# Scores of far keys by residue modulo 4, with a softmax in two parts, in a conformer block on one core

## The chip, the cores and the metric

The kernel runs on one core of a Trainium2 chip. The core has a matrix engine (TensorE, PE in the profile, with its weight loads shown apart as PEld), a vector engine (DVE), a scalar engine (ACT), a general engine (POOL) and a sync engine (SP) that issues most DMA transfers. Each engine works through its own list of instructions in order; they meet by semaphores. The metric is the device time of one execution in microseconds (us), as the median of several runs.

## The reference

One block in float32 on 1024 tokens of 1024 channels: a gated causal convolution branch and an attention branch side by side, their gated sum through `w_out`, then a gated feed-forward part. The attention is what the change touches. It has 16 heads of 64 and three groups (window, dilation); each group has its own softmax, and the three outputs are mixed by the softmax of their log-sums:

```python
DILATION_GROUPS = ((128, 1), (512, 4), (2048, 16))
...
for window, dilation in DILATION_GROUPS:
    o_g, lse_g = dilated_window_attention(q, k, v, slopes, window, dilation)
    outs.append(o_g)
    lses.append(lse_g)
mix = jax.nn.softmax(jnp.stack(lses), axis=0)
o = jnp.einsum('gbsh,gbshd->bshd', mix, jnp.stack(outs))
```

Within a group a query sees the keys whose distance to it is a multiple of the dilation, from 0 up to the window; scores get a linear penalty, slope times distance. Mixing by log-sums makes the three groups one softmax in which a key counts once for each group that holds it. So a query sees every key up to distance 128, every fourth up to 512, and every sixteenth beyond.

## The kernel before

All large products run as three matmuls of 32-bit operands split into a high and a low part (`split`: ACT copies the high part with `Copy`, DVE subtracts it from the source to get the low part). The stages follow each other: normalisation and the first gated products, q, k and v, gates by a block scheme with fewer products, attention, merging, `w_out`, the feed-forward part.

**The attention stage** goes head by head over 128-token query blocks i = 0 to 7. It is one hand-ordered loop (`tc.manual_schedule` for ACT, DVE and PE) over *slots*, one for each head, half and block; eight slots make a head, and `at % 8` is called the *place* here. POOL and SP are not ordered by hand: the scheduler decides their order from the dependences. A slot does, in this order:

- `score`: query block i against the key blocks 0 to i, (i+1) x 128 columns, as two matmuls (high and low part of the keys, `kh` and `kl`; the partitions of `q` hold its high and its low part, 64 each). Then one DVE operation subtracts the score from the mask row, writes the result to `p` in SBUF and its minimum to `st`, with a short readout of that accumulator. One mask tile `m` of 1024 columns a head holds, at a shifted offset for each block, the penalty and the logarithm of the count.
- `share` of the slot before: reciprocal on DVE, then POOL scales `p` by it.
- `fill(FRONT[at % 8])` steps of other work for PE: `gates` is a generator in which each step is three matmuls of 512 columns of a gate or of the convolution's output product. `FRONT` and `BEHIND` hold ten steps a head.
- `flip` for the slot `BACK` = 5 before: PE transposes the 128x128 blocks of one key block into a PSUM bank `pp`, ACT copies to `ph`, DVE subtracts to `pl`. In the second half a slot flips two key blocks.
- `weigh` of what the slot before flipped: two matmuls, values as the stationary operand, into the output bank `o`; after the last, `result` copies `o` out on ACT and SP stores it in two pieces of 128 KB.
- `powers`: ACT takes the exponential of `p` in place with the sum in `st` (and a readout).
- `fill(BEHIND[at % 8])`.

`head(h + 1)` fetches q, kh and kl in six transfers of 256 KB, and the mask, a head ahead into buffers that go in pairs; `values` fetches the values, 512 KB. A key block counts 36 times a head: 1 + 2 + ... + 8. After the last slot come a few slots without scores; there the attention output of the finished half is fetched back for the merge. A DMA's landing is told by one of eight semaphores, and a transfer is issued only when the one that had the same semaphore before it has landed.

The lines of before that the steps name: L911 and L912 scores, L916 mask and minimum with its readout, L921 exponential with its readout, L924 reciprocal, L925 the scaling on POOL, L931 transposes, L82 and L83 the two halves of a split, L945 and L946 weighing, L954 the copy of the output, L956 its stores, L114 to L116 the matmuls of fill steps and other products, L242 and L243 copy and store of the convolution's product, L731 a scaled activation of the convolution branch that writes every second float.

Of the kernel before, what the change touches and what calls it, by code (L numbers as in the profile page):

```python
# [35 lines left out]
FRONT = (1, 1, 0, 0, 0, 1, 0, 1)  # L36
BEHIND = (1, 1, 1, 1, 0, 1, 1, 0)
BACK = 5
# [18 lines left out]
def block_kernel(ctx: ExitStack, tc: tile.TileContext, x, xT, x0, g2, pack, mask,  # L57
# [20 lines left out]
    qkg = cst.tile([P, 1], F32, name="qkg")  # L78

# [74 lines left out]
    dv = [dr.tile([P, 8, 8, P], F32R, name=f"dv{i}") for i in range(2)]  # L154
# [145 lines left out]
    if True:  # L300
# [434 lines left out]
        def head(h):  # L735
# [4 lines left out]
            m = p2.tile([P, T], F32, tag="m", bufs=2, name=f"m_{h}")  # L740
# [73 lines left out]
        with tc.manual_schedule(engines=hand):  # L814
# [4 lines left out]
            for n, (a, b) in enumerate(PAIRS):  # L819
# [25 lines left out]
                act.activation(p5, Y, AF.Copy)  # L845
                if n == 0:
# [43 lines left out]
    if True:  # L890
# [7 lines left out]
        def values(h):  # L898
            vals[h] = p2b.tile([P, 8, P], F32R, tag="v", bufs=2, name=f"v_{h}")
            fetch(vals[h], dv[h // 8][:, h % 8, :, :])  # L900

        def score(h, tiles, i):
            q, kh, kl, m = tiles
            nk = (i + 1) * P
            s = big_ps(f"s_{h}_{i}")

            off = P if nk == 640 else 0
            s = s[:, off : off + nk]
            edges = (0, 512 - off, nk) if nk > 512 else (0, nk)
            for c in map(slice, edges, edges[1:]):  # L910
                pe.matmul(s[:, c], q[:, i * P : (i + 1) * P], kh[:, c], start=True, stop=False)  # L911
                pe.matmul(s[:, c], q[:, i * P : (i + 1) * P], kl[:, c], start=False, stop=True)  # L912
            pt = ready2(f"p{i}", [P, nk], F32, 1, f"p_{h}_{i}")
            st = ready2("st", [P, 32], F32, 4, f"st_{h}_{i}")
            u0 = 896 - i * P
            dve.tensor_tensor_reduce(out=pt, in0=s[:, :nk], in1=m[:, u0 : u0 + nk], scale=-1.0, scalar=3e38,  # L916
                                     op0=ALU.add, op1=ALU.min, accum_out=st[:, 0:1])
            return pt, st
# [3 lines left out]

        def share(pt, st):
            dve.reciprocal(st[:, 2:3], st[:, 1:2])  # L924
            pool.tensor_scalar(pt, pt, st[:, 2:3], 1.0, op0=ALU.mult, op1=ALU.mult)  # L925

        def flip(h, half, pts, kt):
            q0 = max(0, kt - half * 4)
# [735 lines left out]
```

## Time and profile before

| | us |
|---|---|
| runs, three | 1731.17, 1731.82, 1732.20 |
| median | 1731.82 |
| the profiled execution | 1731.03 |
| its span | 1729.2 |
| attention, first score to last weighing | 570 to 911 |

The profile shows one execution. Busy times of an engine are sums of its instructions' spans where these overlap counted once; a matmul's span reaches beyond the start of the next one, since they are pipelined. "Idle before" gives the time in which an engine had nothing to do just ahead of an instruction, and what ended it. The DMA share is the mean busy share of the core's 16 DMA engines. A DMA row shows the time that issuing took; its landing is given apart. A group of instructions has its line, engine, operation, output<-input, shape and count, then busy time in us, mean duration in ns, and idle time before.

### The profile page before, as it was taken

To read this page: it belongs to the slowest core of one execution; us is meant where nothing else is said; L and a number is where in the kernel's file an instruction comes from. 1 tells how busy PE (TensorE), PEld (TensorE's weight loads), DVE (VectorE), ACT (ScalarE), POOL (GpSimd) and SP (SyncE) were. 2 spreads that over 40 slices of the span, in tenths; PEclk is the share of its full clock that TensorE was granted. 3 is DMA by queue.
4 is the path that set the end of the run, shared out by engine and by line. 5 is a ranking of instruction groups with operands and counts; after the bars stand their busy time and mean duration, and the time that the engine had idled before them with its cause. 6 is when DMAs were issued, how large, how long until landed. Compare 5 with 4: busy or idle time off the path is not lost.

```text
span 1729.2 us, 22890 instructions
## 1 busy us (share of the span) xinstructions
PE 1724.0 (100%) x8147; PEld 1438.0 (83%) x8147; DVE 1334.7 (77%) x2034; ACT 810.2 (47%) x1286; POOL 175.5 (10%) x188
## 2 busy tenths in 40 slices
PE   9999999999999999999999999999999999999999
PEld 8888888888888888888888888888888888888887
DVE  5999999999876568777757564787767777889863
ACT  5411233233335567777665542555445444533431
POOL 0000231122000233332220000000000000000000
PEclk9999999999999999999999999999999999999999
DMA  9411145345637967877648685622222222498851
GB/s 374 143 50 49 50 146 166 115 135 168 196 123 230 322 179 223 243 206 205 179 125 319 226 320 191 225 98 86 86 85 74 96 78 83 128 376 306 291 177 49
DMA packets 159987, 299.03 MB, mean 173 GB/s; under 512 B 13312, under 2 KB 63104, under 8 KB 159360
## 3 DMA queue, kind: packets, MB, share of 16 engines
q1 hardware_dynamic: 157424, 291.14, 51.6%
q10 hardware_dynamic: 2448, 6.42, 0.9%
q8 instruction: 64, 1.05, 0.2%
q14 instruction: 51, 0.42, 0.1%
HBM read 213.62 MB, written 83.89 MB: 172 GB/s over the span
## 4 chain that ended last, share of the span: by engine, by line
PE 94%; DMA 3%; DVE 1%; ACT 1%; issue 1%; SPq 0%; ACTq 0%; POOL 0%; DVEq 0%
PE dx L1476 7%; PE xz L138 6%; PE xz L139 6%; PE xz L140 6%; PE dy L1476 5%; PE qkv L133 5%; PE qkv L131 5%; PE qkv L132 5%; PE pp L931 4%; PE y L139 2%; PE y L138 2%; PE y L140 2%; PE o L946 2%; PE s L912 2%; PE s L911 2%; PE o L945 2%
## 5 line engine op out<-in xcount | busy, mean ns | idle before, releaser
L131 PE MATMUL qkv<-hi_qkv,hT 128*128 128x512 f32 x384 | 151.2, 395 | 0.0
L133 PE MATMUL qkv<-hi_qkv,hT 128*128 128x512 f32 x384 | 149.8, 391 | 0.0
L132 PE MATMUL qkv<-lo_qkv,hT 128*128 128x512 f32 x384 | 149.8, 391 | 0.0
L83 DVE TENSOR_TENSOR pl<-pp,ph 128x512 fp32r<-128x512 f32 (+2 forms) x191 | 99.6, 550 | 41.6 <-ACT ph L82 41.3
L82 ACT ACTIVATE ph<-pp 128x512 fp32r<-128x512 f32 (+2 forms) x191 | 86.6, 489 | 76.1 <-PE pp L931 74.5
L916 DVE CUSTOM_DVE_ANT_0 p<-s,m 128x128 f32<-128x128 f32 (+3 forms) x120 | 90.4, 753 | 39.0 <-PE pp L931 21.9
L1379 DVE SCALAR_TENSOR_TENSOR u<-u,pk 128x1023 f32<-128x1023 f32 x88 | 112.1, 1275 | 1.2 <-ACT u L1377 1.0
L925 POOL TENSOR_SCALAR p<-p,st 128x128 f32<-128x128 f32 (+3 forms) x120 | 90.6, 756 | 204.4 <-DVE st L924 174.2
L921 ACT ACTIVATE p<-p,st 128x128 f32<-128x128 f32 (+3 forms) x120 | 93.6, 780 | 8.3 <-DVE st L916 6.0
L107 POOL TENSOR_TENSOR rs<-ss,mhalf 128x8 f32<-128x8 f32 x32 | 66.3, 2074 | 294.7 <-DVE ss L106 294.6
L580 DVE SCALAR_TENSOR_TENSOR cacc<-csum,both,cacc 128x512 f32<-128x512 f32 x120 | 89.2, 743 | 0.3
L580 DVE SCALAR_TENSOR_TENSOR cacc<-apad,pk,cacc 128x512 f32<-128x512 f32 x120 | 88.1, 743 | 0.0
L83 DVE TENSOR_TENSOR lo_uv<-raw_uv,hi_uv 128x1024 fp32r<-128x1024 f32 x20 | 24.5, 1226 | 79.6 <-ACT hi_uv L82 79.6
L133 PEld LDWEIGHTS qkv<-hi_qkv,hT 128*128 128x128 f32 x384 | 72.1, 188 | 15.0
L132 PEld LDWEIGHTS qkv<-lo_qkv,hT 128*128 128x128 f32 x384 | 72.2, 188 | 14.3
L580 DVE SCALAR_TENSOR_TENSOR codd<-apad,pk,codd 128x513 f32<-128x513 f32 x112 | 83.4, 746 | 0.7 <-ACT codd L573 0.7
L131 PEld LDWEIGHTS qkv<-hi_qkv,hT 128*128 128x128 f32 x384 | 72.1, 188 | 14.2
L931 PE MATMUL pp<-ident,p 128*128 128x128 f32 x540 | 79.4, 273 | 0.2 <-POOL p L925 0.2
L931 PEld LDWEIGHTS pp<-ident,p 128*128 128x128 f32 x540 | 64.4, 140 | 11.8 <-POOL p L925 1.1
L945 PE MATMUL o<-ph,v 128*128 128x512 f32 (+2 forms) x191 | 74.1, 391 | 0.0
L138 PE MATMUL xz<-h2left,hi_uv 128*128 128x512 f32 x176 | 68.6, 390 | 0.0
L138 PE MATMUL xz<-blk_t,hi_s3g 128*128 128x512 f32 x176 | 68.5, 389 | 0.0
(441 smaller groups left out, 4960.0 us busy)
## 6 DMA issues: line engine op xcount, KB each, us to landing
wr<-w_down SPq DMA_DIRECT2D x45, 512.0 KB, 5.8
gr<-dff SPq DMA_DIRECT2D x62, 256.0 KB, 5.1
raw_qkv<-w_qkv SPq DMA_DIRECT2D x24, 512.0 KB, 4.3
dff<-u SPq DMA_DIRECT2D x22, 512.0 KB, 2.6
raw_uv<-w_up SPq DMA_DIRECT2D x21, 512.0 KB, 3.3
raw_ug<-w_up SPq DMA_DIRECT2D x20, 512.0 KB, 3.3
dv<-v SPq DMA_DIRECT2D x16, 512.0 KB, 3.3
q<-dq SPq DMA_DIRECT2D x32, 256.0 KB, 5.5
```

What stands on the lines that cost most here:

```text
L83: dve.tensor_tensor(out=lo, in0=src, in1=hi.bitcast(F32), op=ALU.subtract)
L131: pe.matmul(ps, ah, hi[:, k % 2, :], start=(k == 0), stop=False)
L132: pe.matmul(ps, ah, lo[:, k % 2, :], start=False, stop=False)
L133: pe.matmul(ps, al, hi[:, k % 2, :], start=False, stop=(k == KT - 1))
L138: pe.matmul(o, wh[:, k, :], bh[:, k, :], start=(start and k == 0), stop=False, skip_group_check=not start)
L139: pe.matmul(o, wh[:, k, :], bl[:, k, :], start=False, stop=False, skip_group_check=not start)
L140: end = pe.matmul(o, wl[:, k, :], bh[:, k, :], start=False, stop=(k == 3), skip_group_check=not start)
L580: dve.scalar_tensor_tensor(out=out_, in0=src[:, i : i + size], scalar=w(i), in1=out_, op0=ALU.mult, op1=ALU.add)
L931: pe.transpose(pp[:, qb * P : (qb + 1) * P], pts[qb][:, kt * P : (kt + 1) * P], ident)
L945: pe.matmul(o[:, c], v[:, kt, :], ph[:, c], start=(kt == 0), stop=False)
L1379: dve.scalar_tensor_tensor(out=acc[:, d:], in0=src[:, : T - d], scalar=w(2 - d), in1=acc[:, d:], op0=ALU.mult, op1=ALU.add)
L1476: pe.matmul(banks[n][:, cols], a[:, c], b[:, d], start=(start and i == 0 and m == 0), stop=(stop and i == nf - 1 and m == 2), skip_group_c ...
```

## The change

Block i of the second half (i = 4 to 7) no longer scores all of the first half's keys.

- *Near*: blocks 4 to 7 meet keys 512 and up, and block 4 also key block 3 (`lowest`). Blocks 7 and 6 are a unit each, of 512 and 384 columns; 4 and 5 share one bank of 256 + 256.
- *Far*: queries 512 to 1023 meet keys 0 to 511 only where both have the same position modulo 4. For each residue r, the 128 queries and the 128 keys with that residue are taken by access patterns with a step of four floats out of the same `q`, `kh` and `kl` tiles: one 128x128 block each. Block 4's pairs with key block 3 are masked out here. That makes 10 (first half) + 11 + 4 = 25 blocks a head.
- *Softmax in two parts*: near and far have minimum and sum of their own, `own[h]`, with a row for a query. The near part has queries along partitions in order, the far part by residue, so each is written to DRAM (`give`, on ACT's queue, 128x8 floats; the near part in runs of two floats) and read back in the other's layout (`take`, on SP). `combine` then forms the reciprocal of the common sum on DVE (five operations on 128x8, with one exponential on ACT between) and POOL scales the eight pieces.
- *Order*: the second half of a head now comes ahead of the first: far in place 0, then 7, 6, (4, 5), then blocks 3, 2, 1, 0; in the last head the halves are the other way round. `BACK` is 8, `combine` stands in place 6 behind the transposes' splits, `FRONT` and `BEHIND` hold ten steps a head as before, in other places; `START` adds five steps in the first head (before, three were added in the loop), and `TAIL` gives three a slot in the nine slots after the last score (before, four in six).
- *Transposes*: seven groups a head, of 512, 384 and 384 columns for the first half and 512 (far), 512, 384 and 512 for the second, where there were twelve. The columns of near groups are reordered to residue order by the access pattern with which the splits read PSUM, a step of four floats; the far outputs are accumulated into the same bank in runs of 32, and `result` reorders on its way out.
- *Data*: the mask is 640 columns a head; v lies in DRAM by token, and is fetched once in order (runs of 512 bytes) and, its first half, once by residue (`vf`, 256 KB).
- *Buffers*: two score units share a PSUM pair, `p` tiles go in pairs, `ph` and `pl` have three buffers, `ot` two. A small exponential (`warm`) is put at the end of the stage before.

In the built program SP's order in a head in the middle is: the first four fetches of the next head with v of this one among them, two stores of output, the rest of the next head's fetch, its mask and vf, take of the far statistics, take of the near ones, two stores. Fetches of weights and stores of fills come in between.

```diff
-FRONT = (1, 1, 0, 0, 0, 1, 0, 1)
-BEHIND = (1, 1, 1, 1, 0, 1, 1, 0)
-BACK = 5
+FRONT = (1, 1, 1, 0, 0, 0, 1, 1)
+BEHIND = (1, 0, 1, 1, 1, 0, 1, 0)
+BACK = 8
+START = (2, 1, 1, 1, 0, 0, 0, 0)
+TAIL = (2, 1)
...
-                spill(dv[g8][:, :, tt, :], vt.rearrange("p h s d -> p h (s d)"))
+                spill(dv[g8][tt * P : (tt + 1) * P], vt.rearrange("p h s d -> p h (s d)"))
...
+                if n == N - 1:
+                    act.activation(warm, mhalf, AF.Exp)
...
+            fetch(v, dv[h // 8].rearrange("(t p) h d -> p h t d", p=P)[:, h % 8])
+            vf = p2b.tile([P, 4, P], F32R, tag="vf", bufs=2, name=f"vf_{h}")
+            fetch(vf, dv[h // 8][0:512].rearrange("(j r) h d -> j h r d", r=4)[:, h % 8])
...
+        lowest = lambda i: 0 if i < 4 else 3 if i == 4 else 4
+        fourth_of = lambda t, r: t.rearrange("p (j r) -> p r j", r=4)[:, r]
+        by_fourth = lambda t: t.rearrange("p (i a r) -> p i r a", r=4, a=32)
...
+            if units == ("far",):
+                for r in range(4):
+                    scored(s[:, r * P : (r + 1) * P], fourth_of(q[:, 512:], r),
+                           *(fourth_of(t[:, 0:512], r) for t in (kh, kl)))
+                for r in range(4):
+                    pt = whole[:, r * P : (r + 1) * P]
+                    pts[h, "far", r] = pt, own[h][:, 1, r]
+                    least(pt, s[:, r * P : (r + 1) * P], m[:, 512:640], own[h][:, 1, r, 0:1])
...
+        near_of = lambda t: t.rearrange("(i p) c -> p i c", p=P)
+        far_of = lambda t: t.rearrange("(j r) c -> j r c", r=4)
...
+        def give(h, layout):
+            d = dst_[layout][h]
+            act.dma_start((near_of, far_of)[layout](d), own[h][:, layout])
+
+        def take(h, layout):
+            d = dst_[1 - layout][h]
+            sp.dma_start(other[h][:, layout], (near_of, far_of)[layout](d))
+
+        def combine(h):
+            o, t = own.pop(h), other.pop(h)
+            f = ready2("both", [P, 2, 4], F32, 2, f"both_{h}")
+            dve.tensor_tensor(out=f, in0=o[:, :, :, 0], in1=t[:, :, :, 0], op=ALU.subtract)
+            dve.tensor_scalar(f, f, 80.0, None, op0=ALU.min)
+            act.activation(f, f, AF.Exp)
+            dve.tensor_tensor(out=f, in0=f, in1=t[:, :, :, 1], op=ALU.mult)
+            dve.tensor_tensor(out=f, in0=f, in1=o[:, :, :, 1], op=ALU.add)
+            dve.reciprocal(f, f)
+            for r in range(4):
+                times(pts[h, "far", r][0], f[:, 1, r : r + 1])
+            for i in (7, 6, 4, 5):
+                times(pts[h, i][0], f[:, 0, i - 4 : i - 3])
+
+        FLIPS = (((0,), (1,), (2, 3), ()), (("far",), (4,), (5,), (6, 7, 3)))
...
+            order, runs = ((lambda t: t, lambda t: t) if group == ("far",) else
+                           (by_fourth, lambda t: t.rearrange("p (i r a) -> p i r a", r=4, a=32)))
+            split(runs(ph[:, c]), runs(pl[:, c]), order(pp[:, c]))
...
+        SCORES = (((3,), (2,), (1,), (0,)), (("far",), (7,), (6,), (4, 5)))
+        slots = [(h, half, n) for h in range(H) for half in ((1, 0) if h < H - 1 else (0, 1)) for n in range(4)]
...
+                if 0 <= at - 6 < len(slots) and slots[at - 6][1:] == (1, 0):
+                    combine(slots[at - 6][0])
+                for unit in new:
+                    powers(*unit)
+                if cur is not None and half == 0:
                     late = new
+                elif cur is not None and n in (0, 3):
+                    give(h, 1 if n == 0 else 0)
+                    take(h, 0 if n == 0 else 1)
```

More of the change, by code (lines that the diff above doesn't have):

```diff
@@ L78, in block_kernel @@
     qkg = cst.tile([P, 1], F32, name="qkg")
+    warm = cst.tile([P, 8], F32, name="warm")
     def split(hi, lo, src):
@@ L898, in values @@
         def values(h):
-            vals[h] = p2b.tile([P, 8, P], F32R, tag="v", bufs=2, name=f"v_{h}")
-            fetch(vals[h], dv[h // 8][:, h % 8, :, :])
-        def score(h, tiles, i):
-            q, kh, kl, m = tiles
[L904 to L918, printed above, removed]
+            v = p2b.tile([P, 8, P], F32R, tag="v", bufs=2, name=f"v_{h}")
```

163 lines of the change are left out of this document (113 added, 50 removed).

## The prediction, made before the changed kernel was run

> **What bounds the kernel now.** I read the page first, for the engine that fills the span, then the busy times of the attention stage alone, then the chain of waits for the length of a head.
>
> ```profile
> span 1729.2 us, 22890 instructions
> ...
> PE 1724.0 (100%) x8147; PEld 1438.0 (83%) x8147; DVE 1334.7 (77%) x2034; ACT 810.2 (47%) x1286; POOL 175.5 (10%) x188
> ...
> PE 94%; DMA 3%; DVE 1%; ACT 1%; issue 1%; SPq 0%; ACTq 0%; POOL 0%; DVEq 0%
> ```
>
> PE is never idle for long, so work taken from PE is time won, as long as nothing else becomes late. The attention stage in one window (columns: PE, PEld, DVE, ACT, POOL busy, granted clock, DMA share, GB/s):
>
> ```profile
> 600.00:880.00 280.00, 279.74 (x1625) 241.51 (x1624) 204.02 (x546) 204.32 (x478) 85.67 (x114) 1.00 0.72 202
> ```
>
> DVE and ACT are each busy 204 of 280 us (73%), the DMA engines 72%. From the chain, two equal places thirteen heads apart:
>
> ```profile
> 617.35 0.89 PE pp L931 x8
> ...
> 873.22 0.87 PE pp L931 x8
> ```
>
> (873.22 - 617.35) / 13 = 19.68 us a head: at 73%, 14.3 us of ACT and of DVE, and 14.2 us of DMA.
>
> **PE, by the start times of its instructions.** A matmul's duration overlaps the next, so a price is the distance from one start to the next one's (timeline: start, duration).
>
> ```profile
> 801.53 0.33 PE L911 MATMUL s<-kh,q 128*128 128x384 f32 x1
> ...
> 801.70 0.34 PE L912 MATMUL s<-kl,q 128*128 128x384 f32 x1
> ...
> 801.88 0.28 PE L911 MATMUL s<-kh,q 128*128 128x256 f32 x1
> ...
> 802.00 0.28 PE L912 MATMUL s<-kl,q 128*128 128x256 f32 x1
> ...
> 802.12 0.49 PE L931 MATMUL pp<-ident,p 128*128 128x128 f32 x3
> ...
> 802.36 0.47 PE L945 MATMUL o<-ph,v 128*128 128x512 f32 x1
> ...
> 802.67 0.40 PE L946 MATMUL o<-pl,v 128*128 128x512 f32 x1
> ...
> 803.26 0.40 PE L911 MATMUL s<-kh,q 128*128 128x512 f32 x1
> ...
> 803.50 0.40 PE L912 MATMUL s<-kl,q 128*128 128x512 f32 x1
> ...
> 803.73 0.28 PE L911 MATMUL s<-kh,q 128*128 128x256 f32 x1
> ...
> 804.67 0.60 PE L931 MATMUL pp<-ident,p 128*128 128x128 f32 x4
> ...
> 805.35 0.22 PE L945 MATMUL o<-ph,v 128*128 128x128 f32 x1
> ...
> 805.40 0.28 PE L946 MATMUL o<-pl,v 128*128 128x128 f32 x1
> ...
> 805.51 0.44 PE L114 MATMUL ya<-aT,hi_co 128*128 128x512 f32 x1
> ```
>
> A hi and lo pair costs 0.46 us at 512 columns (803.26 to 803.73), 0.35 at 384, 0.24 at 256 and 0.16 at 128 (0.05, then 0.11 until the next starts). A transpose costs 0.11: four took 0.60, of which the last has 0.27. (The first matmul after transposes takes 0.31 instead of 0.23, but starts early by as much.) A fill step is three matmuls of 0.23: 0.69.
>
> Before, a head has scores of 0.16 + 0.24 + 0.35 + 0.46 + 0.59 + 0.70 + 0.81 + 0.92 = 4.23, 36 transposes = 3.96, and weighing by 6, 2, 2, 2 pairs of 512, 384, 256, 128 columns = 4.26: 12.45, and ten fills = 6.9. The sum, 19.35, stands against 19.68 measured.
>
> After, the scores of the first half stay (1.21), tiles 7, 6 and (4, 5) cost 0.46 + 0.35 + 0.48, and the far part is eight matmuls of 128 columns, each with weights of its own. At the 0.16 of a pair they are 0.64, at 0.11 each 0.88. I take 0.88, since in a run of such matmuls no longer one covers the next weights. Sum 3.38. Transposes: 25, 2.75. Weighing: 1.21 for the first half, and 0.88 (far) + 0.46 + 0.35 + 0.24 + 0.32 for the second: 3.46. Together 9.59 (9.11 with the low price), so PE saves 2.86 us a head (up to 3.34), times 16 = 45.8 us. The profiled run took 1731.0 us (median of the runs 1731.8, 0.8 more, inside their spread). If nothing waited, the changed kernel would take 1731.0 - 45.8 = 1685.2.
>
> **What the other engines get.** Rows of the groups kept apart by shape, same window:
>
> ```profile
> L921 ACT ACTIVATE p<-p,st 128x512 f32<-128x512 f32 x15 | 10.9, 725 | 0.0
> L921 ACT ACTIVATE p<-p,st 128x128 f32<-128x128 f32 x14 | 5.5, 394 | 0.0
> L921 ACT ACTIVATION_READ_ACCUMULATOR p<-p,st 128x1 f32 x114 | 22.5, 198 | 0.0
> L82 ACT ACTIVATE ph<-pp 128x512 fp32r<-128x512 f32 x87 | 49.0, 600 | 42.6 <-PE pp L931 41.8
> L82 ACT ACTIVATE ph<-pp 128x384 fp32r<-128x384 f32 x29 | 14.2, 489 | 2.1 <-PE pp L931 1.7 <-ACT ya L242 0.4
> L916 DVE CUSTOM_DVE_ANT_0 p<-s,m 128x512 f32<-128x512 f32 x15 | 10.3, 689 | 6.2 <-PE pp L931 6.2
> L916 DVE CUSTOM_DVE_ANT_0 p<-s,m 128x128 f32<-128x128 f32 x14 | 3.9, 278 | 0.0
> L916 DVE DVE_READ_ACCUMULATOR2_ANT st<- 128x1 f32 x114 | 9.3, 82 | 0.0
> L924 DVE RECIPROCAL st<-st 128x1 f32<-128x1 f32 x114 | 18.0, 158 | 8.3 <-ACT p L921 8.2
> L83 DVE TENSOR_TENSOR pl<-pp,ph 128x512 fp32r<-128x512 f32 x88 | 58.1, 688 | 28.1 <-ACT ph L82 27.8
> L83 DVE TENSOR_TENSOR pl<-pp,ph 128x384 fp32r<-128x384 f32 x28 | 15.2, 544 | 0.2 <-ACT ph L82 0.2
> L925 POOL TENSOR_SCALAR p<-p,st 128x512 f32<-128x512 f32 x14 | 9.7, 696 | 34.3 <-DVE st L924 34.3
> L925 POOL TENSOR_SCALAR p<-p,st 128x128 f32<-128x128 f32 x14 | 5.2, 374 | 5.0 <-PE o L946 4.5
> ```
>
> An exponential is 0.28 us plus 0.11 a block. Eight over 36 blocks were 6.2, twelve over 25 are 6.1: nothing is won. Four more readouts add 0.8. Seven copies for twelve, over 25 blocks for 36, save 1.9 (0.15 + 0.11 a block). The exponential of the combination adds 0.3, and two issues on ACT's queue 0.33 each:
>
> ```profile
> 881.35 0.33 ACTq L243 DMA_DIRECT2D dya<-ya  x1
> ```
>
> ACT stays at 14.2 us, but of a head of 16.8 (19.68 - 2.86): 85%, where it was 73%. Places with many short pieces (0, 3, 4) will now and then hold PE. Bounds 0 and 1 us a head; I take 0.2, that is 3 us, nearer nothing because the excess of one place is made up in the next. DVE falls by 2.5 (minima 0.14 + 0.137 a block: -0.95; splits: -2.1; readouts +0.3; reciprocals -0.6; five small operations of the combination +0.8), to 11.8. POOL shares 25 blocks in twelve pieces, 5.9 us, which costs nothing by itself. Of the rest, v in shorter runs, vf and the narrower mask run on the DMA engines a head ahead of their use; the dv stores and the one exponential (warm) lie in the stages before, beside PE: I take nothing for them. If that cover were gone, warm would cost under 0.39 us and a late v what its landing is over the head that it has.
>
> **The round trip of the statistics** is the wait that the change adds. The near part goes last: give follows the exponentials of (4, 5) in place 3, take is issued when give has landed, and combine asks for it in place 6. What PE does between the score of (4, 5) and the transposes of place 6, in the code's order: 0.44 + 0.35 + 0.69; 0.46 + 0.44 + 0.56 + 0.69; 0.35 + 0.33 + 0.46; 0.24 + 0.69 + 0.33 = 6.0. ACT's and DVE's halves of that split (0.49 and 0.54) make 7.1 until DVE comes to combine. Give is issued after 0.44 of transposes, 0.60 of copy and two exponentials with their readouts (1.4): 2.4. So 4.6 us are left for two transfers. Behind combine stand, on DVE, the minima of places 7 and 0 and the next split, and on POOL eight shares (4 x 0.37 + 0.70 + 0.59 + 2 x 0.48 = 3.7). With five operations of some 0.16 and the exponential the last share ends 4.9 us after combine starts. PE wants it for key block 4 in place 1, after 0.35 + 0.69 + 0.16 + 0.69 + 0.40 + 0.88 + 0.69 + 0.44 + 0.69 + 0.46 + 0.69 = 6.1, less the 1.0 of the split: 5.1. So some 0.2 of slack: a round trip over 4.8 us delays PE by all that it is over.
>
> No transfer this small is in the trace. The nearest are the stores of 128 KB in this window, then the fetch of a head ahead and what follows it:
>
> ```profile
> DMA to landing us min/median/max: 2.5/4.5/8.4
> ```
> ```profile
> 770.30 0.46 SPq L149 DMA_DIRECT2D kh<-dk  x1
> ...
> 774.59 0.53 SPq L745 DMA_DIRECT2D m<-mask  x1
> ```
> ```profile
> 782.00:784.00 2.00, 2.00 (x14) 1.86 (x13) 1.20 (x5) 0.82 (x3) 0.06 (x1) 1.00 0.02 6
> ```
>
> Two at the minimum make 5.0, late by 0.2; two at the median 9.0, late by 4.2. The burst of a head's fetch begins with 770.30 and the DMA engines are empty by 782: 11.7 us. In the changed program SP issues the whole of the next head, with v and vf (0.75 MB more, mask 0.19 less), ahead of both takes; at 202 to 300 GB/s the burst then lasts about 2 us longer and ends near 12 us into the head, when give has just been issued (places 0 to 2 take 2.7 + 2.5 + 2.5, the score 0.5, and 2.4 from there: 10.6). So I choose near the minimum, 3.1 for give at the burst's tail and 2.6 for take: 5.7, late by 0.9, in 15 heads 13.5 us.
>
> [...]
>
> The first head has no transposes or weighing as cover: from its score of (4, 5) to key block 4 PE has 1.4 + 1.15 + 0.35 + 1.6 + 0.85 + 1.6 + 2.3 = 9.2, against 2.4 + 5 + 4.9 = 12.3: 3 us lost. In the last head the tail's three fills a place cover it. Three places more of tail bring the last output fetch closer to the next stage; I put down 1 us (bounds 0 and 3).
>
> **Strided operands.** kh, kl and q of the far scores are read every fourth float. No matmul before reads so. The nearest row is ACT writing every second float, against a contiguous one of as many columns:
>
> ```profile
> L731 ACT ACTIVATE cacc<-cacc,pk x6: 1217/1250/1260, 532.8 to 545.1; 128x1024 f32<-128x1024 f32 x6
> ```
> ```profile
> 909.87 1.07 ACT L82 ACTIVATE hi_ao<-raw_ao 128x1024 fp32r<-128x1024 f32 x1 [0.89 <-DMA raw_ao<-w_ao]
> ```
>
> 1.25 / 1.07 = 1.17. On 0.88 us that is 0.15 a head, 2.4 us in all; the bounds are nothing and a doubling, 14 us. ACT and DVE read the transposes at the same stride, beside PE.
>
> **The sum**: 1731.0 - 45.8 + 13.5 (round trip) + 3 (ACT) + 3 (first head) + 1 (tail) + 2.4 (stride) = 1708.1. Forecast 1708.
>
> **Rivals.** *Nothing waits* (0.12): two transfers of the minimal 2.5 are all but in time and ACT keeps up: 1685 + 2 = 1687. For it: the empty window at 782. Against: ACT at 85% and the longer burst. *Strided reads cost double* (0.12): 14 in place of 2.4, 1720. For it there is only the 17% of ACT's stride of two. [...] *The round trip sets the pace* (0.19): give and take queue behind the burst and DVE, which works in order, stands at combine with the splits behind it. From a lateness of (45.8 - 9.4) / 15 = 2.4 us a head, a round trip of 7.2 us, all is given back. At the median of 4.5 us each it is late by 4.2, 63 us in all, and the kernel takes 1758. For it: that median, and a DMA share that rises to 0.85 or more (14.2 us, and a little more, of 16.8). Against: the takes come when the burst drains. *It comes out even* (0.05): a lateness near 2.4.
>
> **How the numbers follow.** Forecast 0.52, rivals as above. About 0.2%, 3.5 us, is what a measurement tells from no change. The forecast and the first two rivals are faster (0.76), the last but one is slower (0.19). The forecast's own range is 1694 to 1720. The range 1687 to 1738 goes from nothing waiting to the milder cases of the round trip, and leaves out less than 2 in 10.
>
> **What would show it.** Right: a head period of 17.5 to 18 us; transposes at 0.11; far matmuls 0.11 to 0.13 apart; DVE idle some 1 us before the subtraction in combine, released by a DMA, and POOL's shares ending PE's short waits in place 1; ACT near 80%. Wrong: far matmuls 0.2 apart (stride); DVE idle over 2.4 us there (round trip); ACT ending PE's waits in places 0 to 4 by more than 1 us a head; first scores waiting for kh, kl or q, which would mean that the burst itself no longer fits in a head.

## The result, and the profile after

| | before | after |
|---|---|---|
| median of the runs, us | 1731.49 | 1794.11 (1789.98 to 1794.75) |
| ratio, 95% interval | | 1.0356 (1.0338 to 1.0374) |
| first score at, us | 570.2 | 584.7 |
| attention, first score to the first matmul that uses its output, us | 345.3 | 383.3 |
| from there to the last matmul's end, us | 810.5 | 821.7 |

The changed kernel is 3.6% slower. The last three rows are from the profiled executions: 38.0 us of the loss lie in the attention stage; 14.5 lie ahead of it and 11.2 behind it, in stages whose code is as it was but for the order in which v is stored and the small exponential `warm`. In the changed kernel, L916 and L917 are the scores, L959 the exponential, L962 POOL's scaling, L978 give, L982 take, L987 to L992 combine, L1007 the transposes, L1044 and L1045 weighing, L85 and L86 the split. In the runs below the same code can stand some lines off: L913 and L914 are scores in e10 and e11, L959 is POOL's scaling, L975 give and L979 take in e11, and L986, L988 and L997 are the exchange in e13 and e16.

The page of the kernel after: span, busy time of the engines, shares of the chain of waits.

```profile
span 1793.0 us, 22578 instructions
...
PE 1755.0 (98%) x8003; PEld 1434.8 (80%) x8003; DVE 1290.6 (72%) x2098; ACT 786.3 (44%) x1351; POOL 176.6 (10%) x252
...
PE 86%; DMA 9%; ACT 2%; DVE 1%; issue 1%; POOL 1%; SPq 1%; ACTq 0%; DVEq 0%; POOLq 0%
```

PE has 38 us without work (before: 5), and DMA has gone from 3% to 9% of the chain. The attention stage in the window that the prediction used (PE, PEld, DVE, ACT, POOL busy, granted clock, DMA share, GB/s), and four smaller ones:

```profile
600.00:880.00 280.00, 255.21 (x1319) 212.36 (x1318) 148.64 (x547) 163.34 (x478) 75.76 (x151) 0.91 0.83 191
```
```profile
768.00:770.00 2.00, 1.97 (x9) 1.49 (x8) 0.89 (x6) 0.86 (x4) 0.00 (x0) 1.00 0.68 170
770.00:772.00 2.00, 1.14 (x4) 0.62 (x5) 1.74 (x13) 0.82 (x3) 1.84 (x5) 0.77 0.91 184
772.00:774.00 2.00, 2.00 (x7) 1.61 (x7) 0.69 (x1) 1.55 (x6) 2.00 (x5) 0.50 0.98 227
774.00:776.00 2.00, 2.00 (x14) 1.73 (x13) 0.70 (x2) 1.48 (x6) 0.76 (x2) 0.88 1.13 290
```

Every engine does less in these 280 us than before, so none of them is the bound: something makes them wait. Only the DMA engines' share rose, from 0.72 to 0.83; in e6 below it is 0.88 with PE full, so a share as high does not by itself hold PE. And the granted clock, 1.00 before, is 0.91. The small windows show how: PE stops at 770, and then the clock is 0.50 while it works; 7 matmuls start in two microseconds where 14 do later. Such windows last 3.4 or 6.8 us; eleven of them, 54.6 us in all, cost about 27 us of work. Two matmul starts just ahead of such a window were 0.9 to 3.9 us apart (in the unhindered stream .23); about as many gaps of 0.7 to 2.2 us had no window behind them. All eleven windows begin whole multiples of 3.41 us from one another (614.06, 658.43, 678.91 and so on), so they keep to a grid of time; what decides which gap has a window behind it, no run shows.

The waits (engine, output, line, what released it: total us, times, longest):

```profile
DVE both L987 <- DMA other<-dst: 44.8, 16, 5.0
...
PE pp_far L1007 <- POOL pf L962: 20.0, 15, 2.7
...
SPq L982 <- DMA dst<-own: 118.2, 32, 6.8
...
ACT ph L85 <- DMA q<-dq: 5.9, 3, 2.3
```

DVE waits for the take in every head, 2.8 us each (over 2.4 was the prediction's sign for a wrong round trip), and PE behind it for the scaled far part. But SP, which issues the takes, stands 118 us until gives have landed, and even ACT waits until fetches have landed that it does not use. The chain around one head, and the median landings (last number) of two transfers in 640 to 900:

```profile
760.89 6.04 DMA dst<-own
766.99 1.73 DMA other<-dst
768.74 0.18 DVE both L987
...
769.79 0.21 DVE both L992
770.16 0.64 POOL pf L962
```
```profile
dst<-own ACTq DMA_DIRECT2D x24, 4.0 KB, 7.2
other<-dst SPq DMA_DIRECT2D x24, 4.0 KB, 3.7
```

Four kilobytes take 7.2 us to land, more than the 256 KB of `kh` (6.8). Last, two neighbouring far matmuls (start, duration), .23 us apart where the prediction took .11 to .13, its sign for a wrong stride term:

```profile
767.44 0.42 PE L917 MATMUL s_far<-kl,q 128*128 128x128 f32 x1
767.67 0.42 PE L916 MATMUL s_far<-kh,q 128*128 128x128 f32 x1
```

### The profile page after: what moved, and what is told of

The parts are those of the page before. It is cut to its first block, busy times and chain, and to the rows that moved or that the text cites. A ratio compares the mean times of both kernels' runs of the same rounds, so it can differ in the third digit from the quotient of the medians.

```text
span 1793.0 us, 22578 instructions
## 1 busy us (share of the span) xinstructions
PE 1755.0 (98%) x8003; PEld 1434.8 (80%) x8003; DVE 1290.6 (72%) x2098; ACT 786.3 (44%) x1351; POOL 176.6 (10%) x252
## 4 chain that ended last, share of the span: by engine, by line
PE 86%; DMA 9%; ACT 2%; DVE 1%; issue 1%; POOL 1%; SPq 1%; ACTq 0%; DVEq 0%; POOLq 0%
PE dx L1584 7%; PE xz L141 6%; PE xz L142 6%; PE xz L143 6%; PE dy L1584 5%; PE qkv L134 5%; PE qkv L135 5%; PE qkv L136 5%; DMA dst<-own 4%; PE y L141 2%; PE y L142 2%; PE y L143 2%; PE wo L135 2%; PE wo L136 2%; PE wo L134 2%; DMA other<-dst 1%
## 5 line engine op out<-in xcount | busy, mean ns | idle before, releaser
L134 PE MATMUL qkv<-hi_qkv,hT 128*128 128x512 f32 x384 | 153.1, 400 | 0.0
L136 PE MATMUL qkv<-hi_qkv,hT 128*128 128x512 f32 x384 | 151.7, 396 | 0.0
L86 DVE TENSOR_TENSOR pl<-pp,ph 128x512 fp32r<-128x512 f32 (+1 forms) x96 | 59.9, 624 | 80.5 <-ACT ph L85 80.0
L86 DVE TENSOR_TENSOR lo_uv<-raw_uv,hi_uv 128x1024 fp32r<-128x1024 f32 x20 | 24.5, 1225 | 82.4 <-ACT hi_uv L85 82.4
L85 ACT ACTIVATE ph<-pp 128x512 fp32r<-128x512 f32 (+1 forms) x96 | 52.0, 542 | 54.8 <-PE pp L1007 35.6
L142 PE MATMUL xz<-blk_t,hi_s3g 128*128 128x512 f32 x176 | 69.3, 394 | 0.0
L141 PE MATMUL xz<-blk_t,hi_s3g 128*128 128x512 f32 x176 | 69.3, 394 | 0.0
L143 PE MATMUL xz<-blk_t,lo_s3g 128*128 128x512 f32 x176 | 69.0, 392 | 0.0
L141 PE MATMUL xz<-h2left,hi_uv 128*128 128x512 f32 x176 | 68.9, 391 | 0.0
L143 PE MATMUL xz<-h2left,lo_uv 128*128 128x512 f32 x176 | 68.7, 390 | 0.0
L142 PE MATMUL xz<-h2left,hi_uv 128*128 128x512 f32 x176 | 68.5, 389 | 0.0
L1485 ACT ACTIVATE u<-u,pk 128x1024 f32<-128x1024 f32 x44 | 54.5, 1239 | 9.2 <-DVE u L1474 4.5
L920 DVE CUSTOM_DVE_ANT_0 p<-s,m 128x256 f32<-128x256 f32 (+3 forms) x105 | 49.0, 477 | 12.1 <-PE s L917 12.1
```

The lines of the kernel that those rows point to most:

```text
L86: dve.tensor_tensor(out=lo, in0=src, in1=hi.bitcast(F32), op=ALU.subtract)
L134: pe.matmul(ps, ah, hi[:, k % 2, :], start=(k == 0), stop=False)
L136: pe.matmul(ps, al, hi[:, k % 2, :], start=False, stop=(k == KT - 1))
L141: pe.matmul(o, wh[:, k, :], bh[:, k, :], start=(start and k == 0), stop=False, skip_group_check=not start)
L142: pe.matmul(o, wh[:, k, :], bl[:, k, :], start=False, stop=False, skip_group_check=not start)
L143: end = pe.matmul(o, wl[:, k, :], bh[:, k, :], start=False, stop=(k == 3), skip_group_check=not start)
```

## The experiments

Times are medians; "before" in the same sessions was 1731.2 to 1731.8.

| run | us | ratio to before, 95% |
|---|---|---|
| e1_before_warm | 1756.8 | 1.0145 (1.0125 to 1.0165) |
| e18_before_warm256 | 1731.3 | 0.9999 (0.9988 to 1.0009) |
| e2_warm64 | 1792.4 | 1.0339 (1.0307 to 1.0371) |
| e5_no_warm | 1775.4 | 1.0242 (1.0209 to 1.0275) |
| e3_own | 1782.8 | 1.0304 (1.0275 to 1.0332) |
| e15_gives_alone | 1742.2 | 1.0063 (1.0039 to 1.0087) |
| e6_no_round | 1730.6 | 0.9997 (0.9987 to 1.0007) |
| e4_flat | 1792.5 | 1.0358 (1.0337 to 1.0378) |
| e10_one_stride | 1701.6 | 0.9827 (0.9808 to 0.9847) |
| e8_late_act | 1793.8 | 1.0358 (1.0334 to 1.0383) |
| e7_late_sp | 1795.8 | 1.0371 (1.0355 to 1.0386) |
| e9_pool | 1765.9 | 1.0206 (1.0189 to 1.0223) |
| e11_far_last | 1804.1 | 1.0401 (1.0348 to 1.0454) |
| e12_far_last_q | 1807.0 | 1.0437 (1.0418 to 1.0456) |
| e13_pe_exchange | 1765.0 | 1.0194 (1.0177 to 1.0211) |
| e14_pe_exchange_q | 1757.4 | 1.0150 (1.0131 to 1.0170) |
| e16_pe_fp32r | 1726.3 | 0.9967 (0.9956 to 0.9979) |
| e17_pe_fp32r_q | 1721.7 | 0.9944 (0.9929 to 0.9959) |

### A tile of 32 bytes

The stages outside attention had nearly the same instructions, and the same clock, as before. The program lays out its buffers in SBUF from two ends, in left-side and right-side pools. In these stages, matmuls with one operand in a left-side and one in a right-side pool had become slower (`qkv`: from start to start .234 us in the median for .227), those with both on one side had hardly (`dx`: .227 before and after). The one new tile ahead of the left side's others was `warm`.

```diff
+    warm = cst.tile([P, 8], F32, name="warm")            (before + this: e1; [P, 64]: e18)
...
-    warm = cst.tile([P, 8], F32, name="warm")            (after - this: e5)
...
+    warm = cst.tile([P, 16], F32, name="warm")           (after, 64 bytes: e2)
```

> The kernel before, with only the tile `warm` (8 floats, 32 bytes a partition, ahead of the left side's other tiles) and its one Exp added. Theory shift: the tile moves every later tile of the left side by 32 bytes against the right side's, and 512-column matmuls with one operand on each side stand .231 to .235 us apart instead of .227; this costs 25.7 us outside attention (14.5 before the first score, which comes at about 584 instead of 570.2, and 11.2 behind), and some more in the fills inside, so 1755 to 1765 us. Rival: the tile and the Exp cost nothing, as I priced them, and the slower stages have another cause: 1731 within 2 us, first score at 570.

> The kernel after, with `warm` 16 floats long (64 bytes a partition; the Exp still runs over 8). Theory shift with a period of 64 bytes: the relation of left and right tiles is that of before, the stages outside attention fall back to the spacing .227, the first score to 570 us, and the time from 1794 to 1760 to 1769 us. Rival, the tile's size is nothing to it: 1794 within 4 us. Rival, any shift does it, whatever its size: as slow, or slower than 1794.

> The kernel after without the tile `warm` and its Exp, so that left and right tiles stand to each other as before. Theory, the relation of the two operands' addresses modulo 512 bytes sets the spacing of 512-column matmuls (a difference of 0: .227 us; 32: .234; 64: .229 to .233): the stages outside attention run as before, first score at 570, and 1794 falls by 25 to 30 us to 1764 to 1769. Rival, the code's place or the Exp's table load costs it, not the address: over 1785.

> The kernel before with `warm` of 64 floats, 256 bytes a partition (the Exp over 8 of them). It asks for the period of the relation between the two sides' addresses: a shift of 32 bytes gave 1757 and .234 us, one of 64 in the kernel after .229 to .233. If what counts is the difference modulo 256 or a divisor of it above 64: 1731, spacing .227 everywhere, first score at 570. If it is modulo 512 or more: 1740 to 1760, spacing between .229 and .234 where left meets right.

The window 100 to 200 us, in the stage of q, k and v: PE is busy throughout, and the number in its brackets counts the matmuls. Before with 32 bytes more, then with 256 bytes more:

```profile
100.00:200.00 100.00, 100.00 (x430) 80.48 (x430) 91.44 (x130) 20.53 (x24) 0.00 (x0) 1.00 0.15 48
```
```profile
100.00:200.00 100.00, 100.00 (x443) 82.81 (x442) 94.72 (x137) 21.14 (x25) 4.13 (x2) 1.00 0.13 44
```

430 against 443 matmuls at a clock of 1.00: .233 us each for .226. The tile with its one Exp costs 25.0 us in a kernel that is otherwise as before (as expected; in the profiled execution 14.7 ahead of attention, 1.4 in it and 9.7 behind it, which is where the changed kernel lost), and nothing when it is 256 bytes long, with the same Exp. So it is not the Exp but the place that the tile gives the others. By the addresses in the built programs, which no view here shows, the left side's tiles stand 32 bytes further on in e1 than before, 64 in e2 and 256 in e18, and the right side's where they stood. Unshifted, the matmuls with one operand on each side stand .227 us apart; a shift of 32 bytes goes with .234 (the changed kernel), of 64 with .229 to .233 (e2), and with 256 as many start in the window as with none (443). The period of 64 that I expected of e2 was wrong: its first score came at 580.2, and its total moved by under 2 us. Without the tile (e5) the first score is back at 570.6, but the median fell by 18.7 only, to 1775.4 (runs from 1766.4 to 1778.7), where I had expected 1764 to 1769: in the profiled execution attention itself took 7 us more, so that the waits there took back part. By these runs the spacing depends on the tiles' addresses by 3% (.234 for .227); why, none of them shows.

### The way through DRAM

Three runs take parts of it away. In all three, combine uses each part's own statistics twice, so the weights are not those of the whole row.

```diff
-            o, t = own.pop(h), other.pop(h)
+            o, t = own[h], own.pop(h)                     (e3, e15, e6)
...
-                    take(h, 0 if n == 0 else 1)           (e15, e6)
...
-                    give(h, 1 if n == 0 else 0)           (e6)
```

> The kernel after; combine takes each part's own statistics for the other part's too, so that the weights are not those of the whole row; gives and takes are still issued and land. Theory round trip: VectorE no longer waits for a take, TensorE's stops ahead of the far transposes (some 30 us of gaps in 16 heads) go, and with them the windows of 3.4 or 6.8 us in which the granted clock is 0.5 (some 54 us of them, about 27 us lost): 1735 to 1755 us, granted clock 1.00. Rival, the stops are POOL's or ScalarE's own and the windows of half clock come from something else: over 1780, clock still about 0.98.

> The kernel after with its gives on ScalarE but no takes; combine reads each part's own statistics twice, so that the weights are not those of the whole row. Of the 52 us between the run with gives and takes that nobody waits for (1783) and the run with neither (1731), this tells whose standing it is. Theory, ScalarE at the give's issue: 1770 to 1790 us, with TensorE waiting for ph of ScalarE. Rival, SP at the take, which holds back the fetches behind it, and through them the semaphores that ScalarE waits for: 1728 to 1745 us.

> The kernel after with no gives and no takes at all; combine reads each part's own statistics twice, so that the weights are not those of the whole row. It differs from the run in which only the wait of combine was taken away by the 32 stores and 32 loads. Theory, ScalarE stands behind the give's issue, which waits for an older transfer on the same semaphore to land (ScalarE idle 6.8 us before one, TensorE then waits for ph): nothing of it is left, TensorE's clock stays 1.00, attention takes 345.3 - 16 x (2.86 - 1.0) + 3 = 318 us, the time is 1724 to 1738. Rival, ScalarE's or POOL's own load, or the fetches made of more and smaller runs, set the pace: over 1755.

Without the wait in combine 11.3 us are won (1794.1 to 1782.8), with the takes gone another 40.6 (to 1742.2, whose two runs lie 7 us apart), with the gives gone another 11.5 (to 1730.6). Taken away in this order they make 63.5. My expectation for e3 (1735 to 1755) and my theory for e15 (ScalarE's standing) both missed; the larger part goes with the takes, which SP issues, as the rival for e15 had it. How a take gets at PE shows in e3 (ACTq and SPq are issues):

```profile
719.67 0.19 ACT L959 ACTIVATION_READ_ACCUMULATOR pf<-pf,own 128x1 f32 x1
726.27 0.33 ACTq L978 DMA_DIRECT2D dst<-own  x1
726.65 0.63 ACT L190 ACTIVATE hi_co<-raw_co 128x512 fp32r<-128x512 f32 x1 [6.79 <-DMA kh<-dk]
727.18 0.58 ACT L85 ACTIVATE ph<-pp 128x512 fp32r<-128x512 f32 x1
```
```profile
709.31 0.45 SPq L90 DMA_DIRECT2D raw_co<-w_co  x1
714.23 0.33 SPq L982 DMA_DIRECT2D other<-dst  x1
...
718.28 0.59 SPq L152 DMA_DIRECT2D kh<-dk  x1
```
```profile
SPq L982 <- DMA dst<-own: 95.1, 28, 5.6
```

The first fence is ACT's timeline, the second SP's, the third SP's wait at the takes from 600 to 900. The far exponentials end at 719.9 and their give is issued at 726.3: its semaphore is one that a fetch of `kh` had, and that has to land first. A copy of the fill and the split of a transpose stand behind it, and PE stands for the split (for such splits 18.8 us from 600 to 900). That `kh` was issued at 718.3, some transfers behind a take at which SP had stood from 709.8 to 714.2; how much earlier it would have landed without this, no row tells. With both gone, e6:

```profile
600.00:880.00 280.00, 279.67 (x1634) 247.32 (x1633) 178.34 (x657) 199.93 (x585) 91.36 (x184) 1.00 0.88 223
```

PE is full, the clock is 1.00 throughout, and ACT is busy 71%. Attention takes 318.5 us, where I had expected 318.

### The stride

```diff
-                    scored(s[:, r * P : (r + 1) * P], fourth_of(q[:, 512:], r),
-                           *(fourth_of(t[:, 0:512], r) for t in (kh, kl)))
+                    scored(s[:, c], q[:, 512:][:, c], kh[:, c], kl[:, c])          (e4; e10: q for r < 2, kh and kl for the others)
```

> The kernel after; the far scores multiply queries and keys that lie side by side (a block of 128 by a block of 128) instead of every fourth one, which are the wrong ones. Theory stride: the 8 far matmuls of a head fall from .233 to .11 us apart, 1 us a head, 16 us in all: 1776 to 1780 us. Rival, TensorE only waits longer for the statistics instead (the round trip sets the pace): the matmuls are as fast, but the time stays over 1788.

> The kernel without `warm`, without gives and takes (combine as in the run without them), and with far scores of which residues 0 and 1 read the queries side by side and the keys every fourth, residues 2 and 3 the other way round; these multiply wrong keys and queries. Theory, the moving operand's stride alone costs: the matmuls of residues 0 and 1 stand .23 us apart, those of 2 and 3 .11, and the time is 1731 - 26 - 8 = 1697 us, within 4. Rival, the weight load's stride costs it: the same time, the other two slow. Rival, each costs: all .17 to .23, 1705 us.

In e4 the far matmuls stood .11 apart, 1 us a head less, and the time fell by 1.6 us only: PE waited for the statistics instead, as the rival had it. e10 has no round trip and no tile, and shows which operand pays. Six of one head's eight far matmuls, of which the first four have strided keys and contiguous queries, the others the reverse:

```profile
786.10 0.30 PE L914 MATMUL s_far<-kl,q 128*128 128x128 f32 x1
786.22 0.30 PE L913 MATMUL s_far<-kh,q 128*128 128x128 f32 x1
786.33 0.30 PE L914 MATMUL s_far<-kl,q 128*128 128x128 f32 x1
...
786.65 0.40 PE L914 MATMUL s_far<-kl,q 128*128 128x128 f32 x1
786.88 0.40 PE L913 MATMUL s_far<-kh,q 128*128 128x128 f32 x1
787.11 0.40 PE L914 MATMUL s_far<-kl,q 128*128 128x128 f32 x1
```

.11 to .12 apart, then .23. The queries are the weights, so the first of my three answers was wrong and the second, the weight load, held for the matmuls: a stride in the weights doubles the distance, while one in the moving operand costs next to nothing (.118 against .110). The time, 1701.6, is 30 us under before, and just outside the 1697 within 4 that went with it.

### The same transfers from other queues

Five complete kernels give the statistics more time (12 slots from score to transpose for 8, combine 10 slots after the far scores for 6, in e11 and e12 10 for the near and 13 for the far part; values fetched later), and four of them issue them elsewhere; these four also leave out `warm`.

```diff
-BACK = 8
+BACK = 12
...
-            act.dma_start((near_of, far_of)[layout](d), own[h][:, layout])
+            sp.dma_start(...)  or  pool.dma_start(...)    (e7; e9, e11, e12)
...
+                    moves.setdefault(at + 5, []).append((take, h, 0 if n == 0 else 1))    (e9, e11, e12; e8: at + 2, e7: at + 4)
```

> The kernel after, correct, with 12 slots instead of 8 from score to transpose, combine 10 slots after the far scores instead of 6, the take issued 2 slots after its give, the values fetched at place 6; gives are still issued by ScalarE. Theory, ScalarE standing behind the give's issue is a cost of its own: the wait of VectorE for the take is gone, ScalarE's stops are not, 1765 to 1790 us. Rival, only the late arrival of the statistics cost time: 1725 to 1745.

> As the kernel with 12 slots, and besides the gives are issued by SP one slot after the powers (the takes 4 slots after), and `warm` with its Exp is left out. It computes the reference. If the tile, the round trip and ScalarE's stops are the whole loss and the stride alone is left: 1731 - 30 + 3 = 1700 to 1715 us, faster than before. Rival, SP's queue now stands at the gives and the fetches behind it come late: 1735 or more.

> The kernel with 12 slots and without `warm`, correct, with gives (one slot after the powers) and takes (5 slots after) issued by POOL, in the order written out, so that neither ScalarE nor SP stands behind them, and on semaphores of POOL's own that no fetch shares. Theory, the loss beside tile and stride is ScalarE's or SP's standing at a transfer: what is left is the run without gives and takes, less the tile: 1731 - 26 = 1705, between 1700 and 1715 us, faster than before, clock 1.00. [...]

> The kernel with 12 slots, without `warm`, gives and takes on POOL, correct; besides the far part is transposed last of the four groups, each part's weights are combined on their own (near 10 slots after the far scores, far 13), and the subtraction stands one slot ahead of the Exp. The near give has then 10 slots, some 18 us, until its take is used. Theory, what was left (1766 against 1705) is VectorE's wait for takes that POOL gets through 5.6 + 7.1 us after its own turn: gone, 1700 to 1715 us, no pp_far wait over 1 us, clock 1.00. Rival, POOL standing at issues and landings makes its multiplications late whatever the slack: over 1735.

> The same kernel, in which POOL also copies the second half's queries of the next head, residue by residue, into a tile of their own, so that the far scores load contiguous weights and only the keys, the moving operand, have the stride of 16 bytes. Theory, weights alone pay the stride (.234 us against .118 in the run with one stride): far matmuls .118 us apart, 8 x .115 = .92 us a head, 14 us less than the run beside it: 1686 to 1700. [...]

None came near 1705. e8 is just above its first theory (1765 to 1790); e7, e9, e11 and e12 came 51 to 107 us above the upper ends of theirs, e7 and e11 where their rivals had them. In e8 PE's waits for the far part are gone (0.9 us from 600 to 960) and those for ACT's splits are 22.7; ACT stood 4 to 5 us at gives behind `q` and `kl`. In e7 SP stood 158.3 us at the takes, not at the gives as the rival had it. On POOL (e9, e11) the issues, .6 to .8 us each, and the standing ahead of takes hold up POOL's multiplications; e11, POOL's timeline:

```profile
701.03 0.83 POOL L975 DMA_DIRECT2D dst<-own  x1
706.57 0.76 POOL L979 DMA_DIRECT2D other<-dst  x1 [4.71 <-PE s L913]
707.37 0.70 POOL L959 TENSOR_SCALAR p<-p,st 128x512 f32<-128x512 f32 x1
708.04 1.40 POOL L959 TENSOR_SCALAR pf<-pf,both 128x128 f32<-128x128 f32 x4
```

POOL stands 4.7 us before a take whose own give had been issued twelve us earlier, at 694.78, and had landed at 699.31. The row names a score, but the give next to it, issued at 701.03, lands at 706.22, and in the heads from 600 to 760 the take comes .35 or .36 us after that landing each time; by which wait stays open. The far part comes behind it, and PE stands at pp_far 28.6 us in 13 heads. Slack did not help here, where the queue that needs it also waits in order. e12 differs from e11 by POOL's copy of the queries; its mean granted clock is .973 (e11: .971), so its time says nothing of the stride.

### Statistics exchanged on TensorE

These take the transfers out of a complete kernel. Eight 128x128 matrices of zeros and ones bring the statistics into the other layout; a mask and a sum on DVE choose among the four rows.

```diff
+            for l in range(2):
+                for n in range(4):
+                    at = (4 * l + n) * 16
+                    pe.matmul(x[:, at : at + 16], pick[:, 4 * (1 - l) + n], t[:, 1 - l].rearrange("p a b -> p (a b)"),
+                              start=True, stop=True)
...
+            dve.tensor_reduce(out=other[h].rearrange("p l x c -> p (l x) c"), in_=w, axis=AX.X, op=ALU.add)
```

(e16; in e13 the operands are fp32, 8 columns, at place 5. e14 and e17 add POOL's copy of the second half's queries by residue, `qf`.) `warm` is left out in all four.

> The kernel after without `warm`, correct, in which no statistics go through DRAM: at place 5 TensorE multiplies each part's statistics (128x8) by 8 matrices of zeros and ones, 4 for each direction, into 64 free columns of the bank of block 2's scores, VectorE picks the right ones by a mask and a sum, and combine follows at place 6 as in the kernel after. Theory, the whole loss beside tile and stride is the way through DRAM and those who stand at it: 1731 - 26 = 1705, plus 8 small fp32 matmuls a head, of about .09 us by the transposes' spacing, 11.5 us in all: 1709 to 1722, clock 1.00, faster than before. Rival, the exchange needs its time on VectorE too (5 more small operations a head at places with 65 to 70% busy) and TensorE waits for pf again: over 1740.

> The same, and POOL copies the next head's second half of queries, residue by residue, into a tile of its own at place 7, so that the far scores load contiguous weights and only the moving keys have the stride. Theory, the weight load alone pays the stride: far matmuls .118 us apart instead of .234, .92 us a head, 14 us: 1695 to 1708. Rival, the copy on POOL takes it back: within 4 us of the run beside it, or slower.

> The statistics again exchanged by TensorE, correct, but each is first split into a high and a low half of type fp32r (16 columns for 8), so that each of the 8 products is one pass instead of two, and the products stand at place 6, where VectorE has long read the bank that they write into. The run before had 16 passes of .114 us and a stop of 1.1 us a head, 2.9 us x 16 = 46, and the clock at half for 34 us. Theory, these are its whole excess over 1705: passes 8 x .06 to .11 = .5 to .9 us a head, 8 to 14 us, no stop, clock 1.00: 1713 to 1724, faster than before. Rival, many short products with few columns let the granted clock fall by themselves: clock below .995 and over 1730.

> The same with the second half's queries copied residue by residue by POOL (1.15 us a head, on POOL), so that only the far scores' keys have the stride. Theory: far matmuls .118 apart for .234, 8 x .115 x 16 = 14 us less than the run beside it: 1699 to 1712. Rival, the copy delays POOL's multiplications at place 7 ahead of the far transposes: no gain, within 4 us of the run beside it.

PE in e13, around the exchange:

```profile
698.09 0.34 PE L913 MATMUL s<-kl,q 128*128 128x384 f32 x1
699.29 1.06 PE L986 MATMUL s<-own,pick 128*128 128x8 f32 x8 [0.86 <-DVE st L916]
700.20 1.04 PE L988 MATMUL s<-own,pick 128*128 128x8 f32 x8
701.09 0.53 PE L1022 MATMUL pp<-ident,p 128*128 128x128 f32 x3
```

Each of the eight products of two fp32 operands shows as two passes here, sixteen in all, .11 us each (1.8 us), and ahead of them PE waits for DVE to read the bank (0.86 us). The clock was at half for 34 us in all (mean .990). So the time is that of e13's rival, but not its reason: for pf PE waits 0.3 us in the whole stage. e14, with the queries copied so that the far weights are contiguous (.118 apart in e10), takes 7.6 us less than e13, which is still 49 us above its theory (1695 to 1708). In e16 the passes are half as many and stand a place later:

```profile
705.69 0.39 PE L118 MATMUL ya<-aT,lo_co 128*128 128x512 f32 x1
706.38 1.06 PE L997 MATMUL s<-halved,pick 128*128 128x16 f32 x8 [0.30 <-DVE halved L85]
707.29 0.44 PE L1031 MATMUL pp<-ident,p 128*128 128x128 f32 x2
```

.9 us a head; the clock is 1.00, and the kernel takes 1726.3, just above the range that I gave. With contiguous queries (e17) it takes 1721.7, 0.56% (0.41 to 0.71) less than before, and is the fastest that computes the whole; I had expected 1699 to 1712. By distances between starts, scores fell by 14.3 us from e16 to e17, as expected, but transposes rose by 8.9: POOL, with a copy of 1.15 us a head more (e14's row), is later with the far part (PE's weight loads wait for it 12.9 us for 3.8). So 4.6 us were left of 14.

## Why the prediction was wrong

- **PE's saving** was right in the heads and a little less at the ends. In e6, without the round trip, two equal places thirteen heads apart are

```profile
609.19 0.28 PE L916 MATMUL s_far<-kh,q 128*128 128x128 f32 x1
...
840.51 0.43 PE L916 MATMUL s_far<-kh,q 128*128 128x128 f32 x1
```

  so a head takes (840.51 - 609.19) / 13 = 17.79 us for 19.68. The stride, 1.88 us for e4's .89, is still in it; without it 2.88 us a head are saved, and 2.86 was forecast. Over the whole stage, e10 has 310.5 us for 345.3, and with half of the stride still in it, (1.38 - .89) x 16 = 7.8, the saving is 42.6 of the 45.8; the other 3 us are not put down to anything here. **The tail** (1 us): behind the stage PE stands 1.5 us for DVE (`gg`) in the changed kernel.
- **The stride** was mis-sized: 2.4 us by the ratio of a strided write on ACT; measured (.233 - .110) x 8 x 16 = 15.7. The rival "strided reads cost double" had the price (14), and half the reason: by e10 only the weights pay double (.234 for .110), the moving operand .118.
- **The round trip** is the step that failed most. The term was 13.5 us, and what goes with gives and takes is 63.5. "3.1 for give at the burst's tail and 2.6 for take: 5.7, late by 0.9" was 7.2 and 3.7 in the medians. But the wait in combine, the only one that I followed, is worth 11.3 of the 63.5 us. I had priced give's issue on ACT at 0.33 us and the take's on SP at nothing. Behind a take that waits for its give stand the next head's fetches, and behind a give that waits for a fetch's semaphore stand copies and splits. SP's order in a head, and the program's rule that a transfer is issued only when the one before it on its semaphore has landed, were both known, and the sum had no term for them.
- **The clock** was taken as 1.00. Behind about half of its stops PE lost half of another 3.4 or 6.8 us; some 27 of the 63.5 us are of this kind (e6 has no such window). The attention stage as a whole, in the changed kernel and in e6, with the same number of instructions on every engine:

```profile
584.69:968.01 383.32, 351.13 (x1804) 291.00 (x1804) 195.58 (x688) 216.12 (x615) 99.10 (x192) 0.93 0.79 192
```
```profile
584.46:902.95 318.49, 315.97 (x1804) 276.49 (x1804) 195.56 (x688) 216.40 (x615) 98.80 (x192) 1.00 0.86 230
```

  Of the 64.8 us between the two, 29.7 are PE's idle time (32.2 for 2.5) and about 27 the half clock; the other 8 are not put down to anything here.
- **`warm`** at nothing, "under 0.39 us" without cover: 25.0 us (e1). I had priced the instruction and not the tile.
- **ACT at 85%** (3 us): in e6 it is at 71%, and in attention PE waits for it nowhere; the term was not needed. **First head** (3 us): PE's wait ahead of that head's far transposes was 3.5; it is part of the 63.5, and e6 has none.

Together: 1731.8 - 42.6 + 15.7 + 25.0 = 1729.9, and e6, which has these three terms, measured 1730.6. The 63.5 is the difference between the changed kernel and e6, so that adding it tests nothing more. The rival "the round trip sets the pace" forecast 63 us for it by a lateness of 4.2 us at combine in each head; that the number agrees is chance, since the wait there was 2.8 us a head and taking it away is worth a sixth of the 63.5.

## What to carry to other kernels

A transfer's price on an engine's queue is not its issue: ask what its semaphore was used for last and what it waits for, and count everything that stands behind it, on SP too (issuing a take cost .35 us in the changed kernel, and SP stood 118 us ahead of the takes). Where a matrix engine is at 100%, price a stop twice, once for itself and once for the slower clock that followed about half of the stops here. A new tile, however small, moves its neighbours: 32 bytes cost 25.0 us in e1, 256 were free in e18; putting it behind the others was not tried.

## What the runs showed of the hardware that was not expected

- A tile of 32 bytes that shifts one operand's pool against the other's puts matmuls of 512 columns .234 us apart for .227 (the changed kernel); one of 64 bytes .229 to .233 (e2); 256 bytes cost nothing (e18), and 128 were not tried.
- A stride of 16 bytes doubles a run of 128-column matmuls when it is in the weights (.234 for .11), and costs 7% in the moving operand (.118 in e10, against .110 in e4).
- In the changed kernel's attention stage a store of 4 KB, half of the cases in runs of 8 bytes, lands after a median of 7.2 us, a load of as much after 3.7.
- In the changed kernel the granted clock fell to 0.50 for 3.4 or 6.8 us, on a grid of 3.41 us, after gaps between matmul starts as short as 0.9 us, and not after every gap of that length. With e13's sixteen short passes and a gap of 1.1 us a head its mean was .990, with e16's eight 1.000.
